# A two-layer decoder trunk: low parts of the weights on VectorE, a third buffer pair, and the keys' factors in the decay tables

## Chip, cores and metric

The kernel runs on one core of a Trainium2 chip. The metric is the device time of one execution in microseconds, the median of three runs.

## The reference

The input x has 512 rows of 1024 float32 numbers. Layer 0 is a gated DeltaNet, layer 1 a gated short convolution, each between two RMS norms and with a residual.

```python
def reference(x, ...):                       # two layers
    for i in range(2):
        h = rms_norm(x, pre_norm_w[i])
        y = gated_deltanet_mixer(h, ...) if i == 0 else short_conv_mixer(h, ...)
        x = x + rms_norm(y, post_norm_w[i])

def gated_deltanet_mixer(h, ...):
    q, k, v, z, b, a = split(h @ w_in)       # 1024 -> 6176; q, k, v after conv of width 4 and SiLU
    q, k = l2_normalize(q), l2_normalize(k)  # 8 heads of 128, each used by two of the 16 value heads
    beta, g = sigmoid(b), -exp(A_log) * softplus(a + dt_bias)
    o = chunked_gated_delta_rule(q, k, v, g, beta)
    return (rms_norm(o, norm_w) * silu(z)) @ w_out          # 2048 -> 1024
# per head and chunk: A = strict(beta k k^T * decay); u, w = solve(I + A, ...);
# v_new = u - w S;  o = q_dec S + (q k^T * decay) v_new;  S = S * sd + k_dec^T v_new

def short_conv_mixer(h, w_in, conv_w, w_out):
    u, b, c, z = split(h @ w_in, 4)          # 1024 -> 4 x 2048
    return (b * conv3(c * u) * silu(z)) @ w_out             # 2048 -> 1024
```

## The kernel before

Every large product is made from three float32r products: an operand is split into a high part (a cast, `hi`) and a low part (the rest, `lo`), and `mm3` (L179) multiplies hi by hi, hi by lo and lo by hi into one PSUM bank. `weights` (L170) brings a tile of weights: a load into `wraw` on SP's DMA queue (three buffers), then `split` (L162), which casts and subtracts into `whi` and `wlo` (two buffers each). `unit` (L184) makes one column block of 128 outputs for all 512 rows, 24 matmuls.

Layer 0 runs 48 such units over w_in (`in_unit`, L469), four of them written out in the start. Their order is the string at L853: keys, queries, z and values of four groups of four heads each. TensorE's order is the program's order; the other engines are ordered by a planner from priorities. The class `Pump` (L61) keeps a clock of planned TensorE time, and every smaller step is a generator (`c_est`, `c_solve`, `c_q`, `c_delta`, `c_gate`, ...) that yields the planned time until its next step; the table `ADJ` (L44) adds a correction to single yields. `at(-16)` gives weight work a priority 16 us ahead of its unit.

The steps that the change touches:

- The decay tables (`decay_tables`, L413) hold exp of differences of the cumulated decay, one 128x512 tile per head, 16 heads. Group 0's are made in SBUF (tiles `gb`), the others from rows that are read back from DRAM (`gt_d`); all are stored to `dt_d` and loaded again where they are used.
- The key step `c_est` (L552) transposes a key tile, makes its squared norm `ss` and the product `kk` of keys with keys in PSUM, and builds E, minus A of the reference. In group 0 VectorE multiplies kk by the factor `nbp` (minus beta over the norm) and by the table in one pass for each of 128 columns (L591); in groups 1 to 3 ScalarE scales kk (L594) and VectorE multiplies by the loaded table `dt` (L596). E has three buffers, tag "E".
- `c_solve` (L609) inverts the triangular blocks: 31 dependent pairs of small VectorE products (L643, L645), then four TensorE steps (L666, L669, L689, L691).
- `c_q` (L702) makes query times key and multiplies it by the table (L719), and makes `qg` on GpSimd (L724). `c_delta` (L730) is the recurrence over four chunks of 128 rows; it makes u from E (L751), scales it into `Vk` and `Vr` on ScalarE (L757, L760) and adds up the output po (L785, L786). `c_gate` (L796) norms and gates the output; its inverse root is `rsqrt` (L196), a start value on VectorE and three Newton rounds of four GpSimd instructions (L204 to L207) on 128x4 numbers.
- The output projection (`out_products`, L929) runs in 16 tiles per half of the heads, with a third pair of weight buffers `wx` in an E buffer for every third tile. The low parts are GpSimd's in the first half and VectorE's in the second.
- `c_norms` (L966) norms two blocks of 128 rows between the layers: two inverse roots on GpSimd, the residual added on GpSimd (L998), transposes, and a split into `hh` and `hl`.

In the split, GpSimd or VectorE takes the low part:

```python
        eng = nc.gpsimd if pool_lo else nc.vector
        eng.tensor_tensor(out=dst_lo, in0=src, in1=dst_hi.bitcast(F32), op=ALU.subtract)
```

Layer 1 (`short_conv`, L1043, then the products of L1099) takes the high parts on ScalarE and the low parts on VectorE throughout.

## Time and profile before

| what | value |
|---|---|
| median of three runs | 1063.34 us (1060.27 to 1063.79) |
| profiled execution | 1058.4 us, span 1056.7 us |
| mean granted TensorE clock | 0.972 of full |
| busy share of the span | TensorE 93%, VectorE 54%, ScalarE 47%, GpSimd 30% |

Times below come from that one execution. A line number names the line of the kernel that issued an instruction; `split` issues all casts and subtractions from L164, L166 and L168, so there the tile's name tells which work it is. Busy time of an instruction that is held up by another engine's use of the memory counts as busy.

### The profile page before, as it was taken

How to read it: one execution, taken by the hardware profiler on the slowest of the kernel's cores; microseconds unless marked ns; L12 is line 12 of the kernel's file. 1: busy time of each engine (PE TensorE's matmuls, PEld its weight loads, DVE VectorE, ACT ScalarE, POOL GpSimd, SP SyncE). 2: the span in 40 equal slices, each digit the busy share in tenths (PEclk: the TensorE clock that was granted, in tenths of full speed). 3: DMA queues.
4: the chain of work that ended last, by engine and by line, in shares of the span. 5: the costliest groups of instructions: out<-in, count | busy, mean ns of one | idle time of the engine just before them, and what ended most of it. 6: DMA issues, size and time to landing. Idle time of an engine off the chain costs nothing.

```text
span 1056.7 us, 14796 instructions
## 1 busy us (share of the span) xinstructions
PE 979.3 (93%) x5430; PEld 807.9 (76%) x5430; DVE 572.7 (54%) x994; ACT 492.5 (47%) x1106; POOL 318.8 (30%) x518
## 2 busy tenths in 40 slices
PE   7984879996999999999998899999999999999997
PEld 5863657884787778777876799888888888888885
DVE  7599979468625882332156776543334434333233
ACT  4473685683646755465654454323223223332123
POOL 6367643455337543546714520000000000000001
PEclk9887889998999999999999999999999999999999
DMA  6243461245225521586555356533333332333222
GB/s 198 83 140 97 144 217 44 60 123 157 61 60 158 162 75 47 161 274 233 178 183 184 95 158 182 152 87 99 100 90 91 100 100 87 93 99 119 85 96 80
DMA packets 170665, 130.78 MB, mean 124 GB/s; under 512 B 6080, under 2 KB 145984, under 8 KB 170208
## 3 DMA queue, kind: packets, MB, share of 16 engines
q1 hardware_dynamic: 170448, 129.73, 40.5%
q8 instruction: 43, 0.70, 0.3%
q14 instruction: 30, 0.25, 0.1%
q10 hardware_dynamic: 144, 0.09, 0.0%
HBM read 117.16 MB, written 12.65 MB: 123 GB/s over the span
## 4 chain that ended last, share of the span: by engine, by line
PE 61%; DVE 17%; DMA 5%; ACT 4%; POOL 4%; issue 3%; POOLq 0%; SPq 0%; DVEq 0%; ACTq 0%
PE pp L180 14%; PE pp L182 13%; PE pp L181 13%; DVE acc L461 4%; DVE tm L643 3%; DVE Na L645 3%; PE pf L181 2%; PE pf L180 2%; PE pf L182 2%; PE pa L180 2%; PE pa L182 2%; PE pa L181 2%; DMA og_d<-ohs 1%; PE u L751 1%; PE po L786 1%
## 5 line engine op out<-in xcount | busy, mean ns | idle before, releaser
L180 PE MATMUL pp<-hh,whi 128*128 128x512 f32 (+1 forms) x928 | 356.7, 384 | 15.9 <-DVE acc L461 6.3
L182 PE MATMUL pp<-hh,wlo 128*128 128x512 f32 (+1 forms) x928 | 347.3, 374 | 3.0 <-POOL wlo L168 1.6
L181 PE MATMUL pp<-hl,whi 128*128 128x512 f32 (+1 forms) x928 | 346.8, 374 | 1.2 <-DVE r L986 1.2
L166 ACT CAST whi<-wraw 128x1024 fp32r<-128x1024 f32 x151 | 158.6, 1050 | 304.6 <-PE pp L181 169.2
L168 DVE TENSOR_TENSOR wlo<-wraw,whi 128x1024 fp32r<-128x1024 f32 x100 | 125.2, 1253 | 175.0 <-ACT whi L166 173.3
L180 PEld LDWEIGHTS pp<-hh,whi 128*128 128x128 f32 x928 | 177.1, 191 | 50.8 <-issue 10.3
L182 PEld LDWEIGHTS pp<-hh,wlo 128*128 128x128 f32 x928 | 176.8, 191 | 37.4 <-POOL wlo L168 3.2
L181 PEld LDWEIGHTS pp<-hl,whi 128*128 128x128 f32 x928 | 177.3, 191 | 30.4 <-DVE r L986 1.4
L168 POOL TENSOR_TENSOR wlo<-wraw,whi 128x1024 fp32r<-128x1024 f32 x55 | 132.3, 2406 | 113.9 <-ACT whi L166 103.0
L1141 POOL TENSOR_TENSOR ob<-ob,ytNa 128x384 f32<-128x384 f32 x2 | 2.1, 1064 | 421.6 <-ACT ob L1140 421.6
L461 DVE SCALAR_TENSOR_TENSOR acc<-pp,col,acc 128x511 f32<-128x511 f32 (+2 forms) x72 | 53.6, 744 | 16.4 <-ACT acc L458 15.5
L645 DVE TENSOR_TENSOR Na<-Na,tm 128x126 f32<-128x126 f32 (+22 forms) x124 | 52.8, 426 | 3.0
L643 DVE TENSOR_TENSOR tm<-Na 128x126 f32<-128x126 f32 (+22 forms) x124 | 47.2, 381 | 3.0
L181 PE MATMUL pf<-wlo,yh 128*128 128x512 f32 x104 | 41.5, 399 | 0.0
L180 PE MATMUL pf<-whi,yh 128*128 128x512 f32 x104 | 41.0, 394 | 0.0
L182 PE MATMUL pf<-whi,yl 128*128 128x512 f32 x104 | 40.8, 392 | 0.0
L1056 DVE TENSOR_TENSOR cu<-pp,us 128x512 f32<-128x512 f32 (+1 forms) x19 | 11.5, 606 | 47.2 <-PE pp L182 47.2
L180 PE MATMUL pp<-xh,whi 128*128 128x512 f32 x64 | 28.6, 447 | 4.3 <-DVE pn L354 3.7
L461 DVE SCALAR_TENSOR_TENSOR acc<-pn,col,acc 128x511 f32<-128x511 f32 (+2 forms) x24 | 26.2, 1100 | 5.7 <-ACT acc L458 5.5
L724 POOL TENSOR_TENSOR qg<-kq,eg 128x512 f32<-128x512 f32 x16 | 22.3, 1392 | 22.6 <-DMA eg<-gt_d 15.4
L182 PE MATMUL pp<-xh,wlo 128*128 128x512 f32 x64 | 27.1, 424 | 0.0
L181 PE MATMUL pp<-xl,whi 128*128 128x512 f32 x64 | 27.0, 421 | 0.0
(297 smaller groups left out, 1540.4 us busy)
## 6 DMA issues: line engine op xcount, KB each, us to landing
wraw<-in_sw_in_dram SPq DMA_DIRECT2D x76, 512.0 KB, 3.9
wraw<-in_w_in_dram SPq DMA_DIRECT2D x47, 512.0 KB, 3.8
wraw<-in_w_out_dram SPq DMA_DIRECT2D x32, 512.0 KB, 3.4
wraw<-in_sw_out_dram SPq DMA_DIRECT2D x16, 512.0 KB, 3.5
eg<-gt_d SPq DMA_DIRECT2D x16, 256.0 KB, 3.6
dtq<-dt_d SPq DMA_DIRECT2D x16, 256.0 KB, 3.5
gb<-gt_d SPq DMA_DIRECT2D x3, 1024.0 KB, 6.1
dt_d<-gb SPq DMA_DIRECT2D x3, 1024.0 KB, 4.3
```

Of the source, the lines that this page charges most:

```text
L166: nc.scalar.copy(dst_hi, src)
L168: eng.tensor_tensor(out=dst_lo, in0=src, in1=dst_hi.bitcast(F32), op=ALU.subtract)
L180: nc.tensor.matmul(ps, lhsT=lh, rhs=rh, start=start, stop=False)
L181: nc.tensor.matmul(ps, lhsT=lh, rhs=rl, start=False, stop=False)
L182: nc.tensor.matmul(ps, lhsT=ll, rhs=rh, start=False, stop=stop)
L461: nc.vector.scalar_tensor_tensor(out=acc[:, s:], in0=ps[:, :T - s], scalar=w(j), in1=acc[:, s:], op0=ALU.mult, op1=ALU.add)
L643: nc.vector.tensor_tensor(out=tv, in0=N[:, i:i + 1, 0:i].to_broadcast([P, w, i]), in1=X[:, m0:, i:i + 1].to_broadcast([P, w, i]), op=ALU.mult)
L645: nc.vector.tensor_tensor(out=X[:, m0:, 0:i], in0=X[:, m0:, 0:i], in1=tv, op=ALU.add)
L724: nc.gpsimd.tensor_tensor(out=qg, in0=qT, in1=eg, op=ALU.mult)
L751: nc.tensor.matmul(u[:, a], lhsT=gs.E[:, 4 * a + c], rhs=X[:, a] if c else gs.nv[a][:, c], start=True, stop=True)
L786: nc.tensor.matmul(po[:, a], lhsT=gs.qkd[a][:, c], rhs=Vr[:, a], start=c == 0, stop=True)
L1056: nc.vector.tensor_tensor(out=cu[:, h:], in0=pc, in1=us, op=ALU.mult)
```

## The change

- `split` takes the low part on VectorE always. The high part is ScalarE's by default; for the units of the input projection and for all of the output projection it is GpSimd's (`hi_eng=nc.gpsimd`).
- Every third call of `weights` uses a third pair of buffers, `third`: in layer 0 from the time that the table of group 1 is stored (it has the same memory, tag "E3"), in layer 1's input projection from a tile of its own. `unit` asks for its weights at priority -20 instead of -16.
- E has two buffers instead of three; the key step of groups 2 and 3 waits until the recurrence of the group two before is done. The table of group 1 waits for the key steps of group 0.
- In the key step ScalarE multiplies the table in place by beta over the norm (`bp`), VectorE multiplies it by kk, 128x512 at a time, and the scaled table is stored to `dt_d`; so the later loads for the queries bring the factor along, and `Vr` is one plain copy of u. E has the other sign, which the solver takes into account (`subtract`, `minus`).
- Between the layers the inverse roots run on VectorE, with three instructions a round instead of four, and the residual is added on VectorE.
- Some 80 entries of ADJ are set anew; of these a few lines are shown.

```diff
@@ -42 +42 @@
 ADJ = {
...
-    "c_solve0:1": -2.5, "c_solve0:2": 1.5, "c_solve1:1": 15.2, "c_solve2:1": 1.5, "c_solve2:2": -6,
...
+    "c_est00:1": -0.2, "c_est01:1": 9.5, "c_est10:1": 2.5, "c_est21:1": -0.5, "c_est30:1": -1, "c_est31:1": 2.6,
+    "c_norms1:1": 10.1, "c_norms1:2": 3.8, "c_q0:0": 42.6, "c_q0:1": -9.5, "c_q1:0": -0.5, "c_q2:0": 9.6,
+    "c_qnorm30:1": -4, "c_solve0:1": 7.5, "c_solve0:2": 0.8, "c_solve1:1": 42.5, "c_solve1:4": 2.5,
+    "c_solve2:1": 7.9, "c_solve2:2": -6, "c_solve3:1": 5.1, "c_solve3:2": -1.5, "c_v00:1": 4.8, "c_v01:1": 5.1,
...
@@ -159 +162 @@
-    def split(dst_hi, dst_lo, src, pool_lo=False, dve_hi=False):
-        if dve_hi:
-            nc.vector.tensor_copy(dst_hi, src)
-        else:
-            nc.scalar.copy(dst_hi, src)
-        eng = nc.gpsimd if pool_lo else nc.vector
-        eng.tensor_tensor(out=dst_lo, in0=src, in1=dst_hi.bitcast(F32), op=ALU.subtract)
-    def weights(src, pool_lo=False, dve_hi=False, store=None):
+    def split(dst_hi, dst_lo, src, hi_eng=None):
+        (nc.scalar.copy if hi_eng is None else hi_eng.tensor_copy)(dst_hi, src)
+        nc.vector.tensor_tensor(out=dst_lo, in0=src, in1=dst_hi.bitcast(F32), op=ALU.subtract)
+    third, n_w = [], [0]
+    def weights(src, hi_eng=None, store=None):
...
         nc.sync.dma_start(out=raw, in_=src)
+        n_w[0] += 1
+        if store is None and third and n_w[0] % 3 == 0:
+            store = [third[0][:, a].rearrange("p (k n) -> p k n", n=n) for a in range(2)]
         hi, lo = store or (wp.tile([P, kk, n], F32R, tag="w" + t, name="w" + t) for t in ("hi", "lo"))
-        split(hi, lo, raw, pool_lo=pool_lo, dve_hi=dve_hi)
+        split(hi, lo, raw, hi_eng)
@@ -181 +185 @@
-    def unit(src, rhs, t=slice(0, T), pool_lo=False, dve_hi=False):
+    def unit(src, rhs, t=slice(0, T), hi_eng=None):
...
         K, m, n = len(rhs), src.shape[2], t.stop - t.start
-        with at(-16):
-            hi, lo = weights(src, pool_lo, dve_hi)
+        with at(-20):
+            hi, lo = weights(src, hi_eng)
...
-    def rsqrt(pool, y, shape, tag, eng=None):
+    def rsqrt(pool, y, shape, tag, vector=False):
...
                                 op0=ALU.mult, op1=ALU.add)
-        eng = eng or nc.gpsimd
         for _ in range(3):
-            eng.tensor_tensor(out=t, in0=r, in1=r, op=ALU.mult)
-            eng.tensor_tensor(out=t, in0=t, in1=y, op=ALU.mult)
-            eng.tensor_scalar(out=t, in0=t, scalar1=-0.5, scalar2=1.5, op0=ALU.mult, op1=ALU.add)
-            eng.tensor_tensor(out=r, in0=r, in1=t, op=ALU.mult)
+            if vector:
+                nc.vector.tensor_tensor(out=t, in0=r, in1=r, op=ALU.mult)
+                nc.vector.scalar_tensor_tensor(out=t, in0=t, scalar=-0.5, in1=y, op0=ALU.mult, op1=ALU.mult)
+                nc.vector.scalar_tensor_tensor(out=r, in0=t, scalar=1.5, in1=r, op0=ALU.add, op1=ALU.mult)
+            else:
+                nc.gpsimd.tensor_tensor(out=t, in0=r, in1=r, op=ALU.mult)
+                nc.gpsimd.tensor_tensor(out=t, in0=t, in1=y, op=ALU.mult)
+                nc.gpsimd.tensor_scalar(out=t, in0=t, scalar1=-0.5, scalar2=1.5, op0=ALU.mult, op1=ALU.add)
+                nc.gpsimd.tensor_tensor(out=r, in0=r, in1=t, op=ALU.mult)
@@ -248 +256 @@
         xt += [dl.tile([P, T], F32, tag="ktok", name="xtk", bufs=4) for _ in range(2)]
-        sq = [dl.tile([P, 4, T], F32, tag="E", name="sqx", bufs=3) for _ in range(2)]
+        sq = [dl.tile([P, 4, T], F32, tag=t, name="sqx", bufs=n) for t, n in (("E", 2), ("E3", 1))]
@@ -345 +353 @@
         g = sm.tile([P, NH, NC], F32, tag="gg", name="gg", bufs=1)
-        gr = dl.tile([NH, 2, T], F32, tag="E", name="gr", bufs=3)
+        gr = dl.tile([NH, 2, T], F32, tag="E", name="gr", bufs=2)
@@ -426 +434 @@
                     nc.scalar.activation(gb, gb, AF.Exp)
-                    nc.sync.dma_start(out=dt_d[h], in_=gb)
...
             hs = slice(4 * g, 4 * g + 4)
-            tag, nb = ("E", 3) if g == 1 else ("zT", 2)
+            tag, nb = ("E3", 1) if g == 1 else ("zT", 2)
@@ -447 +454 @@
         def c_tables(g):
-            while nunit[0] < 10 + 4 * (g - 2):
+            while groups[0].est < 2 or nunit[0] < 10 + 4 * (g - 2):
...
             decay_tables(g)
+            if g == 1:
+                third.append(dl.tile([P, 2, D], F32R, tag="E3", name="w3", bufs=1))
@@ -469 +478 @@
             first = nunit[0] <= 8
-            ps = unit(w_in_v[:, :, ct * P:(ct + 1) * P], xop if first else hT, pool_lo=True,
-                      dve_hi=nunit[0] < 9)
+            ps = unit(w_in_v[:, :, ct * P:(ct + 1) * P], xop if first else hT, hi_eng=nc.gpsimd)
@@ -551 +559 @@
             g = gs.g
-            while not gates_done or (g > 2 and not groups[g - 3].done):
+            while not gates_done or (g > 1 and not groups[g - 2].done):
...
                 gs.epsa = dl.tile([P, 2, NC], F32, tag="epsa", name="epsa")
-                gs.bp, gs.nbp, gs.bpe = (dl.tile([P, 4, NC], F32, tag=n, name=n) for n in ("bp", "nbp", "bpe"))
-                gs.E = dl.tile([P, 16, P], F32, tag="E", name="E", bufs=3)
+                gs.bp, gs.bpe = (dl.tile([P, 4, NC], F32, tag=n, name=n) for n in ("bp", "bpe"))
+                gs.E = dl.tile([P, 16, P], F32, tag="E", name="E", bufs=2)
@@ -576 +584 @@
             h2, g2 = slice(2 * kh, 2 * kh + 2), slice(4 * g + 2 * kh, 4 * g + 2 * kh + 2)
-            nc.vector.scalar_tensor_tensor(out=gs.nbp[:, h2], in0=beta[:, g2], scalar=-1.0,
-                                           in1=rk2.to_broadcast([P, 2, NC]), op0=ALU.mult, op1=ALU.mult)
+            nc.vector.tensor_tensor(out=gs.bp[:, h2], in0=beta[:, g2], in1=rk2.to_broadcast([P, 2, NC]), op=ALU.mult)
@@ -585 +592 @@
                     nc.sync.dma_start(out=dt, in_=dt_d[h])
-                Eh = gs.E[:, 4 * hl_:4 * hl_ + 4]
                 for c in range(NC):
-                    if g < 1:
-                        last_e = nc.vector.scalar_tensor_tensor(out=Eh[:, c], in0=kk[:, c], scalar=gs.nbp[:, hl_, c:c + 1],
-                                                                in1=dt[:, c], op0=ALU.mult, op1=ALU.mult)
-                    else:
-                        nc.scalar.activation(Eh[:, c], kk[:, c], AF.Copy, scale=gs.nbp[:, hl_, c:c + 1])
-                if g >= 1:
-                    nc.vector.tensor_tensor(out=Eh, in0=Eh, in1=dt, op=ALU.mult)
+                    nc.scalar.activation(dt[:, c], dt[:, c], AF.Copy, scale=gs.bp[:, hl_, c:c + 1])
+                last_e = nc.vector.tensor_tensor(out=gs.E[:, 4 * hl_:4 * hl_ + 4], in0=kk, in1=dt, op=ALU.mult)
+                nc.sync.dma_start(out=dt_d[h], in_=dt)
...
                 fence[:] = last_e, last_sq
-            nc.vector.tensor_scalar_mul(gs.bp[:, h2], gs.nbp[:, h2], -1.0)
@@ -642 +643 @@
                                         in1=X[:, m0:, i:i + 1].to_broadcast([P, w, i]), op=ALU.mult)
-                nc.vector.tensor_tensor(out=X[:, m0:, 0:i], in0=X[:, m0:, 0:i], in1=tv, op=ALU.add)
+                nc.vector.tensor_tensor(out=X[:, m0:, 0:i], in0=X[:, m0:, 0:i], in1=tv, op=ALU.subtract)
@@ -656 +657 @@
             yield ((48, 42, 42, 42)[gs.g],)
+            def minus(act, dst, src):
+                if act:
+                    nc.scalar.activation(dst, src, AF.Copy, scale=-1.0)
+                else:
+                    nc.vector.tensor_scalar_mul(dst, src, -1.0)
@@ -671 +678 @@
                     if stage == 0:
-                        copy(Z[b1], ps[h][b1])
+                        minus(h, Z[b1], ps[h][b1])
@@ -692 +699 @@
                     if stage == 0:
-                        copy(V[up, hs], ps[up])
+                        minus(hf, V[up, hs], ps[up])
@@ -756 +763 @@
                 Vr = dl.tile([P, 4, P], F32, tag="Vr", name="Vr", bufs=1)
-                for a in range(4):
-                    nc.scalar.activation(Vr[:, a], u[:, a], AF.Copy, scale=gs.bp[:, a, c:c + 1])
+                nc.scalar.copy(Vr, u)
@@ -828 +834 @@
                 if c == 0:
-                    gs.oh = dl.tile([P, 4, T], F32R, tag="E", name="oh3", bufs=3)
+                    gs.oh = dl.tile([P, 4, T], F32R, tag="E", name="oh3", bufs=2)
@@ -872 +878 @@
                 after(ins, fence[0])
-                split(hh[:, k], hl[:, k], hf, pool_lo=True)
+                split(hh[:, k], hl[:, k], hf)
@@ -884 +890 @@
             start_h(range(8))
-        with at(10):
-            decay_tables(1)
+        pump.add(c_tables(1))
@@ -923 +928 @@
-        wx = dl.tile([P, 2, 2, 512], F32R, tag="E", name="wx", bufs=3)
-        n_w = [0]
-        def out_products(h0, cs, n, pool_lo):
+        def out_products(h0, cs, n, hi_eng):
...
                 with at(-16):
-                    hi, lo = weights(w_out_v[:, h0 + 2 * kk:h0 + 2 * kk + 2, wide[n]], pool_lo=pool_lo,
-                                     store=(wx[:, 0], wx[:, 1]) if n_w[0] % 3 == 2 else None)
-                n_w[0] += 1
+                    hi, lo = weights(w_out_v[:, h0 + 2 * kk:h0 + 2 * kk + 2, wide[n]], hi_eng)
@@ -943 +944 @@
             for n in range(2):
-                banks = out_products(0, cs, n, True)
+                banks = out_products(0, cs, n, nc.gpsimd)
@@ -985 +986 @@
                 nc.vector.tensor_scalar(out=ms, in0=ms, scalar1=1.0 / D, scalar2=EPS, op0=ALU.mult, op1=ALU.add)
-                return rsqrt(sm, ms, [P, n], "rk")
+                return rsqrt(sm, ms, [P, n], "rk", vector=True)
@@ -995 +996 @@
                                                    op0=ALU.mult, op1=ALU.mult)
-                    nc.gpsimd.tensor_tensor(out=y, in0=y, in1=xr[c, n], op=ALU.add)
+                    nc.vector.tensor_tensor(out=y, in0=y, in1=xr[c, n], op=ALU.add)
@@ -1021 +1022 @@
                 cs = (2 * hf, 2 * hf + 1)
-                banks = out_products(8, cs, n, False)
+                banks = out_products(8, cs, n, nc.gpsimd)
@@ -1039 +1040 @@
             tails = {}
+            third[:] = [sp.tile([P, 2, D], F32R, tag="w3", name="w3", bufs=1)]
@@ -1084 +1086 @@
         pump.prio(0)
+        third.clear()
```

## Rows read from the trace of the kernel before

**Rows 1.** Busy time of each engine by stretch, with granted clock and DMA.

```profile
core 0: us, PE busy (x) PEld busy (x) DVE busy (x) ACT busy (x) POOL busy (x), PEclk, DMA share, GB/s
...
60.00:125.00 65.00, 43.00 (x184) 34.22 (x183) 63.06 (x128) 36.29 (x103) 48.24 (x76) 0.82 0.40 119
125.00:180.00 55.00, 45.13 (x354) 35.16 (x354) 46.35 (x96) 40.02 (x83) 22.13 (x21) 0.94 0.44 138
...
240.00:280.00 40.00, 27.80 (x181) 21.47 (x180) 37.58 (x81) 18.34 (x47) 19.45 (x24) 0.91 0.39 114
280.00:340.00 60.00, 60.00 (x433) 51.96 (x432) 22.22 (x54) 34.91 (x112) 27.65 (x66) 1.00 0.32 93
...
560.00:622.00 62.00, 52.98 (x303) 45.98 (x301) 45.10 (x66) 29.95 (x57) 33.56 (x80) 0.92 0.47 143
622.00:1057.00 435.00, 427.72 (x2033) 354.63 (x2033) 178.72 (x215) 133.84 (x184) 4.12 (x4) 1.00 0.35 105
```

**Rows 2.** TensorE's waits over the span: total us, times, longest us.

```profile
PE kq L712 <- ACT ktok L568: 9.1, 1, 9.1
PE pot L819 <- ACT of L814: 8.8, 1, 8.8
...
PE pp L180 <- ACT zT L528: 5.4, 2, 5.0
...
PE pp L182 <- POOL wlo L168: 1.6, 2, 1.0
```

**Rows 3.** Groups of instructions over the span: busy us, mean ns.

```profile
L166 ACT CAST whi<-wraw 128x1024 fp32r<-128x1024 f32 x151 | 158.6, 1050 | 304.6 <-PE pp L181 169.2 <-issue 64.4 <-PE pf L182 38.6
L168 POOL TENSOR_TENSOR wlo<-wraw,whi 128x1024 fp32r<-128x1024 f32 x55 | 132.3, 2406 | 113.9 <-ACT whi L166 103.0 <-PE tok L536 5.1 <-DVE whi L164 3.3
L168 DVE TENSOR_TENSOR wlo<-wraw,whi 128x1024 fp32r<-128x1024 f32 x100 | 125.2, 1253 | 175.0 <-ACT whi L166 173.3
L461 DVE SCALAR_TENSOR_TENSOR acc<-pp,col,acc 128x511 f32<-128x511 f32 (+2 forms) x72 | 53.6, 744 | 16.4 <-ACT acc L458 15.5
...
L656 POOL COPY E<-Nb 32x512 f32<-32x512 f32 x8 | 4.9, 608 | 12.8 <-DVE Nb L650 12.6
```

**Rows 4.** Groups of VectorE and GpSimd from 60 to 125 us.

```profile
L461 DVE SCALAR_TENSOR_TENSOR acc<-pn,col,acc 128x511 f32<-128x511 f32 (+2 forms) x15 | 17.5, 1176 | 0.0
L645 DVE TENSOR_TENSOR Na<-Na,tm 128x126 f32<-128x126 f32 (+20 forms) x27 | 15.1, 560 | 0.4
...
L168 POOL TENSOR_TENSOR wlo<-wraw,whi 128x1024 fp32r<-128x1024 f32 x5 | 12.4, 2475 | 1.1 <-ACT whi L166 1.1
L168 POOL TENSOR_TENSOR hl<-hf,hh 128x512 fp32r<-128x512 f32 x8 | 11.2, 1410 | 3.5 <-ACT hh L166 3.5
```

**Rows 5.** Timeline of GpSimd, then of VectorE: start us, us, instruction.

```profile
240.41 0.20 POOL L204 TENSOR_TENSOR ft<-fr 128x4 f32<-128x4 f32 x1
...
247.56 2.34 POOL L168 TENSOR_TENSOR wlo<-wraw,whi 128x1024 fp32r<-128x1024 f32 x1
...
253.22 0.20 POOL L207 TENSOR_TENSOR fr<-fr,ft 128x4 f32<-128x4 f32 x1
...
247.29 0.26 DVE L645 TENSOR_TENSOR Na<-Na,tm 128x96 f32<-128x96 f32 x1
247.58 2.45 DVE L643 TENSOR_TENSOR tm<-Na 128x115 f32<-128x115 f32 x1
```

**Rows 6.** Timeline of GpSimd in the norms between the layers.

```profile
562.52 0.19 POOL L204 TENSOR_TENSOR rkt<-rkr 128x2 f32<-128x2 f32 x1 [31.41 <-DVE rkr L200]
...
566.63 0.20 POOL L207 TENSOR_TENSOR rkr<-rkr,rkt 128x2 f32<-128x2 f32 x1
567.69 7.32 POOL L998 TENSOR_TENSOR ytNa<-ytNa,xr 128x512 f32<-128x512 f32 x4 [0.87 <-DVE ytNa L996]
```

**Rows 7.** Group 2's key step, group 0's end, group 2's first use, a table load.

```profile
L594 ACT ACTIVATE E<-kk,nbp x16: 346/379/409, 209.7 to 227.1; 128x128 f32<-128x128 f32 x16
...
230.56 0.39 PE L786 MATMUL po<-Vr,qkd 128*128 128x128 f32 x2
...
L751 PE MATMUL u<-nv,E x8: 275/275/377, 379.6 to 380.9; 128*128 128x128 f32 x8
...
dt<-dt_d SPq DMA_DIRECT2D x12, 256.0 KB, 2.9
```

24 rows, old and new, of the table ADJ are left out of this document.

## The prediction

> **What bounds the kernel now.** I read the stages first: the table of busy time by stretch [rows 1]. From 622 us to the end TensorE is busy for 427.72 of 435 us at full clock, and the missing 7.3 us are the drain behind its last product. Nothing in the change can shorten that part, so the whole question lies in the first 622 us, the DeltaNet layer and its output projection. There the idle time of TensorE sits in four stretches: 22.0 us in 60 to 125, 9.9 in 125 to 180, 12.2 in 240 to 280 and 9.0 in 560 to 622 (length less busy time). In the same stretches the granted clock falls to 0.82, 0.94, 0.91 and 0.92 of full, so they pay twice. VectorE is busy for 63.06 of 65 us in the first and 37.58 of 40 in the third, but for only 22.22 of 60 in 280 to 340: it limits in patches, not on average.
>
> Second, TensorE's own waits [rows 2]. The long ones end at ScalarE (a key copy that holds a PSUM bank, 9.1 us; the scaled output before the gate's transpose, 8.8; the gate z, 5.4). For a low part of a weight it waits only 1.6 us in all. So the weights are not late as such. What is late are short jobs that stand behind long ones.
>
> Third, why they are late. When GpSimd subtracts a low part, VectorE's small solver product stands still: one that takes 0.26 us takes 2.45 at 247.58, and GpSimd's pass runs from 247.56 for 2.34 us [rows 5]. GpSimd pays as well: its chain of small Newton steps for the output norm starts at 240.41 and ends at 253.42, with two of these long passes between its links; TensorE's 8.8 us wait ends right behind it. In 60 to 125 this is summed up in [rows 4]: 15 convolution passes from SBUF take 17.5 us where those from PSUM take 0.744 each [rows 3], so 6.3 us too much; 27 solver updates take 15.1 us where 0.27 each would be 7.3, so 7.8 too much. That is 14.1 us of stretching beside 23.6 us of GpSimd passes (wlo and hl), or 0.6 us for each us.
>
> **The change part by part.**
>
> *The weights' split.* By the code 44 units of the input projection and 16 tiles of the output projection move their low part from GpSimd (2.406 us each) to VectorE (1.253), and these 60 and 16 more move their high part from ScalarE (1.050; four from VectorE) to GpSimd [rows 3]. No row shows that cast on GpSimd. From below, its copy of 512 elements takes 0.608, and an equal time for 1024 is the least; from above stands its own subtraction, 2.406. I take twice the copy, 1.2 us, because the cast too reads one operand. Per unit the chain cast, subtract becomes 1.2 + 1.25 = 2.45 us instead of 1.05 + 2.41 = 3.46, and ScalarE loses 1.05 us per unit.
>
> For VectorE in 60 to 125: five low parts (6.3 us) and eight of the normalised input come to it, each of these half as long, 0.63 (5.0), in sum 11.3 us. GpSimd's passes fall from 23.6 to 6.0 us (five casts), so 0.6 x 17.6 = 10.6 us of stretching go: +0.7 for VectorE.
>
> *Keys' factors in the decay tables.* In the first group 16 small VectorE passes, 0.27 us each if they are like the solver's, become four products of 512 elements (0.63): 4.3 become 2.5 us, and half of the 1.8 saved lies in 60 to 125. In the others ScalarE scales the table instead of the PSUM product, as many passes as before; only it can now start before the product is there. The recurrence's four scaled copies become one, on ScalarE, off the state's own path. So VectorE's account of 60 to 125 closes at -0.2; with the five casts gone from ScalarE's queue, where the key copy stands, I take -2. Bounds: +10 (no stretching goes) and -10 (all 14.1 us of it go, so -3.7 on VectorE, and half of the 11.7 us by which the clock of 0.82 shortens these 65). Twelve more 256 KB stores go through the in-order SP queue, behind which the next table and weight loads stand; and as two table buffers serve four heads, the third load of a group waits until the first store has landed. A load of that size takes 2.9 us [rows 7]; three groups that pay it in full are 8.7. I put +1 on it, since the recurrence that needs the tables starts much later (next but one), bounds 0 and +9.
>
> *125 to 180.* The 5.4 us for z ends at ScalarE; a cast less on its queue gives 1 us. The solver's TensorE steps, which wait in the rest of the stretch, are placed later for groups 0 and 1, with weight products before them. I take -4 of 9.9, bounds 0 and -8; VectorE's added passes, six or seven low parts, fit into its 8.7 us of idle time here.
>
> *240 to 280.* The Newton chain loses 2 x (2.34 - 1.2) = 2.3 us directly. More matters that the key buffer E goes from three to two: the key step of group 2 now waits for the end of group 0's recurrence. It ran from 209.7 to 227.1; that recurrence ends at 230.6 [rows 7]. So the solver's 62 dependent steps behind it move by some 21 us, into the stretch where VectorE is busy a third of the time. It costs nothing, as group 2's recurrence first reads E at 379.6. I take -7 of 12.2 and the clock's 3.6 (0.09 of 40), bounds 0 and -13.
>
> *Third buffer pair.* It gives a unit's time of reserve. Directly it can save the 1.6 us of [rows 2]; I take -2 with the shorter chain, bounds 0 and -6 (with what is late in stretches not named here). In the second layer nothing waits.
>
> *Norms between the layers.* Twelve GpSimd steps from 562.52 to 566.83 become nine on VectorE; at the same 0.28 us a step that is 2.5 instead of 4.3. Four residual adds of 7.32 us [rows 6] become four VectorE passes of 0.63, 2.5 us. Twice, once per half of the rows, that is some 13 us of chain; the stage has only 9.0 us idle and 5 us of lost clock (0.08 of 62). The second half's casts go to GpSimd, which is otherwise free there. I take -6, bounds 0 and -12.
>
> *Sum:* -2 - 4 - 7 - 2 - 6 + 1 = -20. The profiled execution took 1058.4 us (span 1056.7 and 1.7 around it), so 1038.4; the median of the runs lies 4.9 above that execution, which gives **1043 us**.
>
> **The rivals.**
>
> *The exchange is empty.* If a GpSimd cast blocks VectorE as the subtraction did, a unit takes 1.2 + 1.25 = 2.45 us of the two engines' common time instead of 2.41, and ScalarE's cast, which stopped nobody, is wasted. Then only norms and placement remain, half as strong: 1054 to 1066, say 1060. For it speaks the stretched row of [rows 5]; against it, that VectorE then waits 1.2 us at a time and not 2.4, and that the small chains pass sooner. The Trainium skill states this rule on the page "SBUF — State Buffer", section "SBUF: two separate sides": GpSimd and a VectorE instruction with two SBUF inputs take a shared port pair exclusively for a whole instruction, and ScalarE never waits on anyone. The trace agrees in its first half (0.26 us became 2.45). By "GPSIMD Engine Reference", section "Engine selection", one-input work runs near line rate; at that page's 1.2 GHz 1024 elements are an estimated 0.85 us, by which the stretching in 60 to 125 would fall by 1 us more.
>
> *VectorE becomes the bound (slower).* Place: the stretches where it has no idle time, above all 60 to 125. It decides if the cast takes long: the first stage breaks even where 0.6 x (23.6 - 5c) = 11.3 - 0.9, at c = 1.25 us, barely over my 1.2. In 60 to 125, 125 to 180 and 240 to 280 some 15 low parts and 8 of the input bring 24 us; if half of it delays TensorE, the time is 1075, if all, 1087.
>
> *The placement does more.* If the steps placed later take away nearly all 53 us of idle time in the four stretches, beyond the waits for VectorE, 1005 to 1022, say 1015. Against it: 60 to 125 has no VectorE time to spare.
>
> **How the numbers follow.** Forecast (1022 to 1054) 0.55; more gain 0.13; empty exchange 0.14; slower 0.18. A change under 0.3% (3.2 us) can't be told from none, so the same is 1060.1 to 1066.5. Faster: 0.55 + 0.13 and 0.05 of the empty exchange, 0.73; same 0.09; slower 0.18. The range 1018 to 1070 leaves out about half of the biggest gain and some two thirds of the slower case, 0.2 together.
>
> **What would show it.** Right: low parts on VectorE near 1.25 us and casts on GpSimd near 1.2; solver steps no longer stretched to 2.4; the wait of 8.8 us gone; group 2's key step behind 231 us; the stretch of the norms without GpSimd; the second layer at the same 435 us. Wrong: casts over 1.25 us, VectorE full to 180 us with more TensorE idle time than 22.0 and 9.9, a key or query step that waits for a table load, or new waits of TensorE at the moved steps.

## The result, and the profile after

The changed kernel takes **1029.99 us** (median; 1027.09 to 1035.51), the kernel before on the same chip 1063.36; the ratio is 0.9698 with an interval of 0.9652 to 0.9744, so some 33 us faster. The forecast was 1043 in a range of 1018 to 1070. The profiled execution took 1028.76 us, 9.6 less than the 1038.4 of the sum. Its busy time by stretch, with the columns of [rows 1]:

```profile
60.00:125.00 65.00, 47.17 (x217) 38.30 (x218) 60.01 (x127) 42.27 (x126) 38.13 (x69) 0.84 0.53 162
125.00:180.00 55.00, 52.66 (x403) 42.34 (x403) 49.37 (x110) 32.21 (x82) 13.62 (x20) 1.00 0.51 154
240.00:280.00 40.00, 37.34 (x180) 30.82 (x179) 31.32 (x78) 24.09 (x83) 13.40 (x41) 0.96 0.41 119
...
560.00:592.00 32.00, 29.14 (x211) 27.14 (x210) 30.81 (x74) 16.33 (x31) 0.00 (x0) 0.95 0.61 169
592.00:1027.00 435.00, 428.07 (x2040) 354.72 (x2038) 178.07 (x217) 133.69 (x185) 4.08 (x4) 0.99 0.36 104
```

The last 435 us are as before, so all of the gain lies ahead of them. TensorE's idle time (length less the first column) is 17.8, 2.3, 2.7 and 2.9 us in the four stretches that had 22.0, 9.9, 12.2 and 9.0. The first hardly looks better, but stretches of equal clock time no longer hold equal work. So I laid both traces' matmuls out in order, gave each the usual interval of its line in the trace of before, and read when each kernel reached the same sum (worked out, no view of the profile):

```
time in before, us       125   180   240   300   560   622
time after, same work  119.3 164.8 224.2 277.1 534.0 592.0
gain so far              5.7  15.2  15.8  22.9  26.0  30.0
```

Half of the gain is made by 180 us. How far one execution can be trusted is shown by e10 below, in which every engine has the same order. The same sums from its trace, of an execution of 1033.82 us, give gains of 3.2, 12.3, 13.1, 19.4, 22.7 and 24.4 at these six points; so a single stretch is known to some 3 us. TensorE's remaining waits in 60 to 125 (what waited, for what; us in all, times, longest):

```profile
PE pp L184 <- POOL w L166: 8.4, 1, 8.4
PE pp L184 <- DVE pn L362: 5.8, 1, 5.8
PE pp L186 <- DVE w L167: 3.9, 1, 3.9
```

The costs that the forecast had to estimate, in groups by line (count | busy us, mean ns), from the lists of VectorE and GpSimd:

```profile
L166 POOL CAST whi<-wraw 128x1024 fp32r<-128x1024 f32 x51 | 62.1, 1219 | 94.0 <-PE pp L185 60.8 <-PE pa L186 16.2 <-DMA wraw<-in_w_out_dram 6.5
L166 POOL CAST w<-wraw 128x1024 fp32r<-128x1024 f32 x25 | 28.6, 1142 | 43.9 <-PE pp L185 25.0 <-PE pa L186 8.0 <-DVE rkr L210 5.9
...
L646 DVE TENSOR_TENSOR Na<-Na,tm 128x126 f32<-128x126 f32 (+22 forms) x124 | 39.4, 317 | 2.7
L644 DVE TENSOR_TENSOR tm<-Na 128x126 f32<-128x126 f32 (+22 forms) x124 | 37.5, 302 | 2.9
L470 DVE SCALAR_TENSOR_TENSOR acc<-pn,col,acc 128x511 f32<-128x511 f32 (+2 forms) x24 | 17.6, 745 | 5.5 <-ACT acc L467 5.3
```

The cast takes 1.14 to 1.22 us in the mean, as taken (1.2); its median is 1.045, and a few that VectorE holds up are longer. The solver's pairs took 426 + 381 ns in the kernel before and take 317 + 302: 124 pairs, 23 us of VectorE's time.

```profile
L645 DVE TENSOR_TENSOR Na<-Na,tm 128x126 f32<-128x126 f32 (+22 forms) x124 | 52.8, 426 | 3.0
L643 DVE TENSOR_TENSOR tm<-Na 128x126 f32<-128x126 f32 (+22 forms) x124 | 47.2, 381 | 3.0
```

The convolution passes that took 1.1 us in the kernel before are back at 745 ns. A cast does hold VectorE up, but shortly. In the changed kernel's timeline a product that is free at 0.28 takes 1.01 us beside a cast of 1.14, where one beside a subtraction took 2.45 [rows 5]:

```profile
113.39 1.14 POOL L166 CAST whi<-wraw 128x1024 fp32r<-128x1024 f32 x1
...
113.35 0.28 DVE L644 TENSOR_TENSOR tm<-Na 128x126 f32<-128x126 f32 x1
113.67 1.01 DVE L646 TENSOR_TENSOR Na<-Na,tm 128x126 f32<-128x126 f32 x1
```

### The profile page after: what moved, and what is told of

Same layout as the page of the kernel before. It is cut to its first block, busy times and chain, and to the rows that moved or that the text cites. A ratio compares the mean times of both kernels' runs of the same rounds, so it can differ in the third digit from the quotient of the medians.

```text
span 1026.6 us, 14732 instructions
## 1 busy us (share of the span) xinstructions
PE 974.4 (95%) x5430; PEld 805.7 (78%) x5430; DVE 612.3 (60%) x1100; ACT 420.6 (41%) x1002; POOL 235.4 (23%) x446
## 4 chain that ended last, share of the span: by engine, by line
PE 75%; DVE 9%; DMA 6%; ACT 4%; issue 3%; POOL 2%; SPq 0%; POOLq 0%; DVEq 0%; ACTq 0%
PE pp L184 17%; PE pp L186 17%; PE pp L185 17%; PE pf L185 3%; PE pf L184 2%; PE pf L186 2%; PE pa L186 2%; PE pa L185 2%; PE pa L184 2%; PE u L758 2%; DVE wlo L167 1%; DMA gb<-gt_d 1%; PE po L792 1%; PE psn L772 1%; PE p L748 1%
## 5 line engine op out<-in xcount | busy, mean ns | idle before, releaser
L184 PE MATMUL pp<-hh,whi 128*128 128x512 f32 (+1 forms) x624 | 239.2, 383 | 5.1 <-DVE acc L470 2.1
L185 PE MATMUL pp<-hl,whi 128*128 128x512 f32 (+1 forms) x624 | 233.3, 374 | 1.0 <-DVE r L987 1.0
L186 PE MATMUL pp<-hh,wlo 128*128 128x512 f32 (+1 forms) x624 | 233.3, 374 | 0.0
L167 DVE TENSOR_TENSOR wlo<-wraw,whi 128x1024 fp32r<-128x1024 f32 x115 | 141.4, 1229 | 135.5 <-ACT whi L166 110.1
L166 ACT CAST whi<-wraw 128x1024 fp32r<-128x1024 f32 x64 | 67.2, 1050 | 189.8 <-PE pp L185 112.2
L186 PEld LDWEIGHTS pp<-hh,wlo 128*128 128x128 f32 x624 | 118.8, 190 | 22.2
L185 PEld LDWEIGHTS pp<-hl,whi 128*128 128x128 f32 x624 | 119.1, 191 | 21.1 <-DVE hl L167 1.2
L184 PE MATMUL pp<-hh,w 128*128 128x512 f32 (+1 forms) x304 | 116.1, 382 | 0.0
L186 PE MATMUL pp<-hh,w 128*128 128x512 f32 (+1 forms) x304 | 113.2, 373 | 1.1 <-DVE w L167 1.1
L185 PE MATMUL pp<-hl,w 128*128 128x512 f32 (+1 forms) x304 | 113.2, 372 | 0.0
L166 POOL CAST whi<-wraw 128x1024 fp32r<-128x1024 f32 x51 | 62.1, 1219 | 94.0 <-PE pp L185 60.8
L167 DVE TENSOR_TENSOR w<-wraw,w 128x1024 fp32r<-128x1024 f32 x50 | 62.6, 1252 | 33.8 <-ACT w L166 31.7
L186 PEld LDWEIGHTS pp<-hh,w 128*128 128x128 f32 x304 | 57.3, 189 | 12.4 <-DVE w L167 1.5
L184 PEld LDWEIGHTS pp<-hh,w 128*128 128x128 f32 x304 | 57.5, 189 | 10.3 <-issue 0.4
```

Of the source, the lines that this page charges most:

```text
L166: (nc.scalar.copy if hi_eng is None else hi_eng.tensor_copy)(dst_hi, src)
L167: nc.vector.tensor_tensor(out=dst_lo, in0=src, in1=dst_hi.bitcast(F32), op=ALU.subtract)
L184: nc.tensor.matmul(ps, lhsT=lh, rhs=rh, start=start, stop=False)
L185: nc.tensor.matmul(ps, lhsT=lh, rhs=rl, start=False, stop=False)
L186: nc.tensor.matmul(ps, lhsT=ll, rhs=rh, start=False, stop=stop)
```

## The experiments

Each starts from the changed kernel unless it says otherwise; a loss in us is the difference of its ratio to 0.9698, times the 1062 us of before. Lines of "..." in a diff stand for edited lines that are not shown.

**The split's engines put back, and the high parts on ScalarE.**

In e1 the low parts are GpSimd's and the high parts ScalarE's (the first four VectorE's) where the kernel before has them so; in e2 only the high parts move, to ScalarE:

```diff
e1
-        nc.vector.tensor_tensor(out=dst_lo, in0=src, in1=dst_hi.bitcast(F32), op=ALU.subtract)
+        (lo_eng or nc.vector).tensor_tensor(out=dst_lo, in0=src, in1=dst_hi.bitcast(F32), op=ALU.subtract)
-            ps = unit(..., xop if first else hT, hi_eng=nc.gpsimd)
+            ps = unit(..., xop if first else hT, hi_eng=nc.vector if first else None, lo_eng=nc.gpsimd)
-                split(hh[:, k], hl[:, k], hf)
+                split(hh[:, k], hl[:, k], hf, lo_eng=nc.gpsimd)
...
e2
-            ps = unit(..., xop if first else hT, hi_eng=nc.gpsimd)
+            ps = unit(..., xop if first else hT)
-                banks = out_products(8, cs, n, nc.gpsimd)
+                banks = out_products(8, cs, n, None)
...
```

> The changed kernel with the split's engines put back: low parts of the input projection, of the normalised input and of the first half of the output projection on GpSimd, high parts on ScalarE (the first four units' on VectorE). All else stays as changed: steps placed anew, third pair, factors in the tables, norms. If the exchange of engines is the main source of the 33 us (theory 'exchange'): 1045 to 1055 us, solver products of VectorE stretched to over 2 us again, mean of the solver's two products back above 0.37 us. If the new placement is the main source (theory 'placement'): 1025 to 1036 us. If it is the third pair: also 1025 to 1036 us.

> The changed kernel with all high parts on ScalarE and all low parts on VectorE, so GpSimd casts nothing. If a GpSimd cast stops VectorE as its subtraction did (the rival 'empty exchange' in its weaker form): 5 to 10 us faster, 1020 to 1025 us, since some 76 casts of 1.2 us no longer meet VectorE. If ScalarE's queue is the dearer place, because 76 casts of 1.05 us stand there behind table passes and gate work: 1032 to 1040 us.

Measured: e1 1057.18 us, ratio 0.9952 (0.9938 to 0.9965), a loss of 27 us. e2 1056.86, 0.9947 (0.9924 to 0.9970), 26 us. Both lie above every value expected. In e1 the first stage is far worse (same columns as above), with a wait of TensorE of 14.8 us for the first tile of the third pair:

```profile
60.00:125.00 65.00, 40.70 (x178) 32.46 (x179) 57.08 (x113) 44.21 (x120) 43.95 (x72) 0.76 0.40 121
125.00:180.00 55.00, 46.29 (x307) 36.23 (x307) 42.28 (x100) 38.22 (x80) 25.00 (x21) 0.88 0.58 183
```

```profile
PE pp L184 <- DVE w L166: 14.8, 1, 14.8
```

VectorE is busy for less than in the changed kernel (57.08 of 65, then 42.28 of 55), and TensorE idles 24.3 and 8.7 us. But these 65 us hold less work. For the TensorE work that the changed kernel does from 60 to 125, e1 takes from 59 to 140, and there VectorE is busy for 68.8 us against 60.0, with 13 more of the solver's products done:

```profile
59.00:140.00 81.00, 50.57 (x218) 40.15 (x218) 68.78 (x135) 53.15 (x138) 55.33 (x82) 0.79 0.45 137
```

So the sum of VectorE's busy time doesn't tell the two kernels apart. By equal work e1 has lost 20 of its 27 us by 161 us. In e2 GpSimd casts nothing, and the solver runs almost free (groups by line):

```profile
L644 DVE TENSOR_TENSOR tm<-Na 128x126 f32<-128x126 f32 (+22 forms) x124 | 34.2, 276 | 2.8
L646 DVE TENSOR_TENSOR Na<-Na,tm 128x126 f32<-128x126 f32 (+22 forms) x124 | 33.3, 269 | 2.9
```

A ScalarE cast holds VectorE up by nothing that shows: 19 products that run beside one, and beside no GpSimd instruction, take 259 ns in the mean, and 176 beside neither take 252 (worked out from e2's trace, no view). GpSimd's casts cost these products 9 us in all ((302 + 317 - 276 - 269) x 124). Still e2 loses 26 us; in its trace 8 by 161 us and 33 by 424. TensorE's waits from 55 us on that end at ScalarE come to 28 us against 9 in the changed kernel (those at GpSimd to 0 against 8, at VectorE to 30 against 20), so a good part of it is lost in ScalarE's queue; what the displaced order adds is not separated. The empty exchange falls, and so does the idea that the cast would be as well on ScalarE.

**Old places, and the new split alone in the kernel before.**

e3 has the table ADJ of the kernel before and nothing else put back. Of the 83 entries in the changed table, 24 have another value than before and 17 are new, and three are gone; the other 42 stayed, so fewer were set anew than the "some 80" above. e7 is the kernel before with the new split alone (and `pool_lo` on in the second half of the output projection):

```diff
e7, against the kernel before
...
-        eng = nc.gpsimd if pool_lo else nc.vector
-        eng.tensor_tensor(out=dst_lo, in0=src, in1=dst_hi.bitcast(F32), op=ALU.subtract)
+        (nc.gpsimd.tensor_copy if pool_lo else nc.scalar.copy)(dst_hi, src)
+        nc.vector.tensor_tensor(out=dst_lo, in0=src, in1=dst_hi.bitcast(F32), op=ALU.subtract)
...
```

> The changed kernel with the table of corrections of the kernel before, so only the placement of the steps goes back. Theory 'placement': 1045 to 1060 us, with the waits of TensorE at the solver's and the gate's steps back. Theory 'exchange': 1030 to 1040 us.

> The kernel before with the new split alone: casts on GpSimd, low parts on VectorE in the units of the first layer and in the output projection, and the low parts of the normalised input on VectorE; places, two buffer pairs, tables and norms as before. Theory: split and places are worth something only together. The solver's TensorE steps stand where the solver's products on VectorE were just done with the old split, and VectorE has now more work ahead of them, so TensorE waits for them as in the changed kernel with the old places: 1070 to 1090. Rival, the forecast's addition: the split alone takes 10 to 15 us away by less stretching of VectorE, 1047 to 1055.

Measured: e3 1083.25 us, 1.0200 (1.0179 to 1.0220); e7 1083.68, 1.0202 (1.0178 to 1.0226). Both are 21 us slower than before, and e3 is slower than either theory had it. TensorE's longest waits, of e3 and then of e7:

```profile
PE pz L670 <- DVE X L651: 29.7, 4, 10.9
PE pot L822 <- ACT of L817: 11.3, 3, 5.8
```

```profile
PE pz L661 <- DVE X L648: 19.7, 3, 10.4
PE pot L814 <- ACT of L809: 16.1, 5, 6.1
```

The solver's first TensorE step (pz) now comes before VectorE has finished X. By equal work e7, in which only the split is new, is 16.4 us *ahead* of the kernel before at its 173 us; at 316 us 1.5 are left, at 627 it is 21.4 behind. So the split by itself lets TensorE run ahead. But the solver is not ahead as far: its products for group 1 end at 170.7 us in e7, at 177.9 in the kernel before, so 7 us sooner, and at the old place TensorE stands for them:

```profile
172.64 1.92 PE L661 MATMUL pz<-X,E 32*32 32x32 f32 x64 [10.44 <-DVE X L648]
```

In the changed kernel these products end later still, at 185.5; there the step stands at 194, behind more weight products (the entry `c_solve1:1` goes from 15.2 to 42.5), and doesn't wait. That is what the new places do for the split at this step. Long waits of e7 stand also at the gate (pot) and at the norms between the layers, 10.8 us in one. The old split at the new places (e1) is 27 us slower than the changed kernel and 5 faster than the one before, and the norms alone give 4.6 (e11, below). So split and places give little or a loss alone.

**The third pair: used late, only in the output projection, or its table freed early.**

```diff
-        if store is None and third and n_w[0] % 3 == 0:
+        if store is None and third and n_w[0] % 3 == 0 and n_w[0] > 3:
e5
+        if store is None and third and n_w[0] % 3 == 0 and kk == 2:
e9, in decay_tables
-                        if g == 1:
+                        if g == 0:
                             after(e, fence[1])
```

The first is e4. In e9 the fence falls away: with g == 0 the function has returned before this line. In e5 `kk == 2` holds for the output projection's tiles alone.

> The changed kernel, but the third buffer pair is first used at the sixth weight tile instead of the third, so that no unit waits for the store of group 1's table, which has the same memory. In the changed kernel TensorE waits 8.4 us for the cast into that pair and 3.9 us for its low part, at 72 to 86 us. If this wait is a loss of its own: 1017 to 1024 us and no wait of over 3 us there. If VectorE, busy for 60 of the 65 us from 60 to 125, is the bound there and the wait is only where its lateness shows: 1027 to 1032 us, with the idle time moved behind 90 us.

> The changed kernel, but the third pair of weight buffers serves the output projection alone, as before; the units of both layers' input projections take the two pairs. If the third pair is the small reserve of the forecast (2 us), the median is 1030 to 1034 us, and the waits of TensorE for a low or high part grow by a few us in all. Rival: with a chain of GpSimd cast and VectorE subtraction that stands behind other VectorE work, the third pair is what lets the units run ahead; then waits for weights appear in many stretches of the first 500 us and the median is 1040 or more. In the second layer both expect no difference in the 435 us.

> The changed kernel without the fence that holds one of the sixteen exponentials of group 1's table until the second key step's squares are made. In the changed kernel that one runs at 74.38, alone, between two table loads of 1.28 us; the store of the table and with it the third weight pair's first use stand behind it, and TensorE waits 8.8 and 4.5 us at that tile. The planner then also pulls group 1's key products on VectorE ahead of the solver's. If that wait is a loss of its own, the median falls by 4 to 10 us, to 1020 to 1026. Rival, after the run that used the pair later: VectorE and the order of its work set the end of the first 180 us, and what is gained before 90 us is given back behind it: 1028 to 1045.

These go back to the largest wait left, 8.4 us (and 3.9 behind it). One exponential of group 1's table is held by a fence and runs alone at 74.38 (ScalarE's timeline of the changed kernel); the store behind it delays the cast into the third pair, which has the same memory (GpSimd's timeline):

```profile
54.63 4.50 ACT L448 ACTIVATE gb<-gb,nG 128x128 f32<-128x128 f32 x15
61.48 1.28 ACT L472 ACT_TABLE_LOAD   x1
73.08 1.28 ACT L448 ACT_TABLE_LOAD   x1
74.38 0.40 ACT L448 ACTIVATE gb<-gb,nG 128x128 f32<-128x128 f32 x1
74.80 1.28 ACT L472 ACT_TABLE_LOAD   x1
```

```profile
79.19 1.48 POOL L166 CAST w<-wraw 128x1024 fp32r<-128x1024 f32 x1 [1.63 <-DMA dt_d<-gb]
```

Measured: e4 1037.27 us, 0.9761 (0.9730 to 0.9792), 7 us lost; e9 1037.18, 0.9759 (0.9734 to 0.9785), 6 lost; e5 1039.83, 0.9798 (0.9772 to 0.9824), 11 lost. The intervals of e4 and e9 touch that of the changed kernel, which ends at 0.9744, but not that of its repetition e10, which ends at 0.9722. e4 lies above both of its expected ranges. In e4 and e9 the wait is gone, and by equal work they are 13 and 15 us ahead where the changed kernel is at 93 us. At its 161 us they are 6.4 and 0.7 behind, at 204 us 13.2 and 6.1. In their place stand other waits for VectorE; in e9:

```profile
PE pp L184 <- DVE acc L470: 8.5, 3, 4.5
PE pp L184 <- DVE pn L362: 6.3, 1, 6.3
```

That wait was therefore no loss that its removal gives back: my theory of 1017 to 1026 fell twice. In e5 low parts are late in many places (`PE pp L186 <- DVE wlo L167: 11.6, 6, 3.5` in its waits).

**The norms and the keys' factors put back, and the norms alone in the kernel before.**

e8 also stores group 0's tables where they are made, as before; e11 is e6 the other way round, in the kernel before.

```diff
e6
-                return rsqrt(sm, ms, [P, n], "rk", vector=True)
+                return rsqrt(sm, ms, [P, n], "rk")
-                    nc.vector.tensor_tensor(out=y, in0=y, in1=xr[c, n], op=ALU.add)
+                    nc.gpsimd.tensor_tensor(out=y, in0=y, in1=xr[c, n], op=ALU.add)
e8
...
-                    nc.scalar.activation(dt[:, c], dt[:, c], AF.Copy, scale=gs.bp[:, hl_, c:c + 1])
-                last_e = nc.vector.tensor_tensor(out=gs.E[:, 4 * hl_:4 * hl_ + 4], in0=kk, in1=dt, op=ALU.mult)
-                nc.sync.dma_start(out=dt_d[h], in_=dt)
+                    if g < 1:
+                        last_e = nc.vector.scalar_tensor_tensor(out=Eh[:, c], in0=kk[:, c], scalar=gs.bp[:, hl_, c:c + 1], in1=dt[:, c], ...)
+                    else:
+                        nc.scalar.activation(Eh[:, c], kk[:, c], AF.Copy, scale=gs.bp[:, hl_, c:c + 1])
+                if g >= 1:
+                    nc.vector.tensor_tensor(out=Eh, in0=Eh, in1=dt, op=ALU.mult)
...
-                nc.scalar.copy(Vr, u)
+                for a in range(4):
+                    nc.scalar.activation(Vr[:, a], u[:, a], AF.Copy, scale=gs.bp[:, a, c:c + 1])
```

> The changed kernel, but the inverse roots and the residual between the layers are GpSimd's as before. If the term of the forecast (6 us) is right, the median is 1034 to 1038 us and TensorE's busy share from 560 us to the start of the second layer falls by about 5 us of work. Rival: the other work of that stretch hides the longer chain, or GpSimd's casts for the second half hide behind it: 1029 to 1032. Second rival: with these casts on the same engine the residuals of 7 us delay the weights as well, and it costs 8 to 12 us: 1038 to 1042.

> The changed kernel, but with the keys' factors applied as before: in the first group VectorE multiplies by factor and table in 16 small passes, in the others ScalarE scales the product of the keys, the tables are stored without the factor, and the recurrence scales four copies. If this part is worth what the forecast put on it (about nothing, one us of it on VectorE in 60 to 125), the median is 1029 to 1034. Rival: the first group's key step sets the end of 60 to 125, and its 16 small passes and the four scaled copies per chunk are a good part of what the change gave: 1038 to 1045, with the loss before 150 us and in the recurrences.

> The kernel before with the norms between the layers on VectorE alone, nothing else. Put back in the changed kernel they cost 12 us, all of it at one wait for the second block's transposes. If they are worth that by themselves, the median is 8 to 12 us under before, 1050 to 1055; if the forecast's term holds, 6 us, 1055 to 1058; rival: in the kernel before the work of the second half of the output projection hides most of the chain, and it gives 0 to 3 us.

Measured: e6 1042.18 us, 0.9812 (0.9787 to 0.9837), 12 lost, by equal work all of it behind 529 us, where one wait stands out: TensorE stands 13.6 us before the transposes of the norms, behind four residual adds on GpSimd of 6.27 us together and two chains of 12 steps:

```profile
PE pxr L1011 <- DVE hs L1005: 13.6, 1, 13.6
```

```profile
552.23 6.27 POOL L999 TENSOR_TENSOR ytNa<-ytNa,xr 128x512 f32<-128x512 f32 x4 [0.87 <-DVE ytNa L997]
558.46 0.20 POOL L212 TENSOR_TENSOR rkt<-rkr 128x1 f32<-128x1 f32 x1
```

e11 1058.06, 0.9957 (0.9941 to 0.9973): in the kernel before the same edit gives 4.6 us. On VectorE a step takes 0.16 us, not the 0.28 of the forecast. e8 1043.62, 0.9832 (0.9809 to 0.9855), 14 lost, but not where I had put it: until 295 us it is up to 3 us ahead, and 8 us of the loss appear at one step of group 2's solver, for which VectorE is 5.7 us late (the granted clock is 0.76 from 295 to 316 us there):

```profile
306.35 3.67 PE L702 MATMUL pdw<-X,E 64*64 64x64 f32 x32 [5.68 <-DVE X L690]
```

**The scale: the same program again, and places off by 1 us.**

```diff
e10, in unit
-        with at(-20):
+        with at(-16):
e12
-    "c_delta0:0": -2.5, "c_delta0:10": 2.1, "c_delta0:14": 4, "c_delta0:3": -1, "c_delta0:9": 1.3,
+    "c_delta0:0": -1.5, "c_delta0:10": 1.1, "c_delta0:14": 5, "c_delta0:3": -2, "c_delta0:9": 2.3,
...
```

> The changed kernel with the units' weights asked for 16 us ahead instead of 20, as before. The forecast put nothing on this edit. If each order of the steps is about as good as another, the median stays at 1028 to 1034. Rival: the table of corrections is set for one order of the engines' queues, and any edit that shifts the order costs about what the third pair, the keys' factors and the norms cost when they were put back one at a time: 1036 to 1044.

> The changed kernel with nothing but its table of places disturbed: each of the 83 corrections is moved by 1 us, in turn up and down. It is the scale for the runs that put one part back: each of these also moves the steps around it. If the order need not be exact to 1 us, the median stays within 3 us of the changed kernel (1027 to 1033), and the 10, 12 and 14 us that the third pair, the norms and the keys' factors cost when put back are the parts' own. If the order is set to within 1 us, it costs 6 to 15 us (1036 to 1045), spread over many short waits, and a part's price read by putting it back alone is an upper bound that holds such displacement.

Measured: e10 1029.32 us, 0.9696 (0.9670 to 0.9722). The edit leaves the order on every engine as it was, so this is a repetition, and agrees to 0.0002. e12 1053.88, 0.9919 (0.9887 to 0.9951): 23 us lost by moving 83 corrections by 1 us each, more than the 15 that were the most expected. Waits of TensorE in e12, and GpSimd's timeline at the longest wait for the gate's transpose (pot):

```profile
PE pot L825 <- ACT of L820: 16.9, 5, 6.5
PE pp L184 <- POOL w L166: 10.4, 1, 10.4
```

```profile
434.26 0.20 POOL L213 TENSOR_TENSOR ft<-ft,fy 128x4 f32<-128x4 f32 x1
437.77 1.26 POOL L731 TENSOR_TENSOR qg<-kq,eg 128x512 f32<-128x512 f32 x1 [3.32 <-DMA eg<-gt_d]
439.00 0.19 POOL L214 TENSOR_SCALAR ft<-ft 128x4 f32<-128x4 f32 x1
439.13 1.04 POOL L166 CAST whi<-wraw 128x1024 fp32r<-128x1024 f32 x1
440.13 0.20 POOL L215 TENSOR_TENSOR fr<-fr,ft 128x4 f32<-128x4 f32 x1
```

Between two 0.2 us steps of the output norm's root stands a pass that waits 3.3 us for a table load. Nothing of the work has changed; only what stands behind what in a queue. By equal work e12 has lost 4 us at 161 us, 12 at 295 and 25 at 529. The waits for pot come to 4.0 us in the changed kernel and 16.9 here, so short waits there are one thing that the places buy.

So e1 reads in two parts, for its 27 us in all are hardly more than the 23 of e12. By 161 us e1 has lost 20. A displacement of the order has cost 4 by then in e12, and between 1 and 9 in the others that keep the new split on its engines (e3, e4, e5, e8, e9). So at least some 11 of the 20 are the split's, and e7 shows 16 in the same stretch from the other side. Its later loss, some 9 us, is no more than a displacement costs. The 11 and 14 us of e5 and e8 lie within that too and can't be read as these parts' own prices.

## Why the prediction was right, and what was mis-sized

- **The bound.** Right: the second layer stayed at 435 us, all gain lies in the first layer and its projection, and VectorE's stretched short jobs are short again.
- **The split, 60 to 180 us.** The terms were -2 and -4; by equal work the gain is 5.7 by 125 us and 9.5 in 125 to 180 (3.2 and 9.1 in e10's trace). The second is outside its own bound of -8, which left out the 3.3 us that the granted clock of 0.94 cost there (it is 1.00 after). These two terms are 9.2 of the 9.6 us between sum and trace; they are what was mis-sized. The prices in them held (cast, low part; the low parts of the input take 0.82, not 0.63). What was wrong is the place of the longest wait. The forecast put the 9.1 us for the key copy down to ScalarE's queue, from which five casts go. But ScalarE itself had just stood 5.7 us for a convolution pass of VectorE (ScalarE's timeline of the kernel before):

```profile
105.43 0.63 ACT L463 ACTIVATE kq<-acc 128x512 f32<-128x512 f32 x1 [5.66 <-DVE acc L461]
107.42 0.58 ACT L568 COPY ktok<-tok 128x512 f32<-128x512 f32 x1
```

  So most of this wait was VectorE's. TensorE's waits in 60 to 180 for the key copy, for the convolved keys (tok on kq, 8.1 us, which the forecast doesn't name) and for z come to 22.6 us before; with the split alone (e7, 58 to 163 us, the same work) 3.6 are left, in the changed kernel 0.8. They are not the split's alone to remove: in e1, with the old split, new places and the other parts leave 5.9. The balance of VectorE's busy time, with break-even at a cast of 1.25 us, was close by its own numbers (the casts in 60 to 125 took 1.19 to 1.24). It left out the short steps of the norms and the keys' factors, which were stretched too (0.88 and 0.80 us before, 0.17 and 0.16 in e7, some 4 us in all), and it doesn't say what TensorE waits for. How long single short steps are held up differs clearly between the two splits (2.45 us beside a subtraction, 1.01 beside a cast).
- **240 to 280 us.** -7 forecast, 7.1 by equal work from 240 to 300. Group 2's key step runs at 238 us, behind the end of group 0's recurrence, and TensorE doesn't wait for its solver; "at no cost" is right, though without much reserve: in e8 the same solver is 5.7 us late. The forecast named only the two low parts between the links of the Newton chain. Two `qg` passes stood there as well, each behind a wait for its table (kernel before):

```profile
244.27 1.38 POOL L724 TENSOR_TENSOR qg<-kq,eg 128x512 f32<-128x512 f32 x1 [1.16 <-DMA eg<-gt_d]
251.52 1.42 POOL L724 TENSOR_TENSOR qg<-kq,eg 128x512 f32<-128x512 f32 x1 [1.44 <-DMA eg<-gt_d]
```

  With the waits they are 5.4 us of the chain's 13, more than the low parts' 4.7, and the change leaves such passes between the links.
- **Third pair and the rest to 560.** -2 forecast, 3.1 by equal work. Right in size; new is the 8.4 us wait for its memory, which the list of what would show it wrong named as a new wait, and whose removal in e4 and e9 gains nothing.
- **Norms.** -6 forecast; 4.0 by equal work, 4.6 in e11. The forecast's sum of 13 us counts one inverse root for each half of the rows where there are two. That e6 loses 12 I put down to the work placed ahead of it, which no run separates.
- **Table stores.** +1 forecast. None of TensorE's waits of 1.5 us or more ends at a table load itself, but the longest one left for the gate stands behind two. It ends behind a Newton chain from 219.66 to 230.66 us, in which two `qg` passes wait 3.38 and 1.15 us for their tables (changed kernel; the first of them, then TensorE):

```profile
223.52 1.29 POOL L731 TENSOR_TENSOR qg<-kq,eg 128x512 f32<-128x512 f32 x1 [3.38 <-DMA eg<-gt_d]
231.11 1.26 PE L825 MATMUL pot<-ident,of 128*128 128x128 f32 x4 [3.62 <-ACT of L820]
```

  The sign named as wrong shows on the other engines too. ScalarE's scaling in the key step waits 7.1 us for its tables (nothing before), VectorE's query products 8.9 (2.4), `qg` 20.6 in all (15.4). So the term is not nothing; how much of these waits the added stores cause stays open.
- **Rivals.** The empty exchange had the mechanism right: a cast also holds VectorE up. The Trainium skill, "SBUF — State Buffer", section "SBUF: two separate sides", says so for a GpSimd instruction that reads there, against a VectorE instruction with two inputs from there, and says that ScalarE never waits on anyone. The trace agrees with the first by the 1.01 us beside a cast, and with the second by the 259 ns beside a ScalarE cast in e2. The rival's price was wrong, since a cast holds for half as long. The slower case did come, in e3 and e7, at 1083 us and by another mechanism than the one I gave: not VectorE full to the end, but TensorE's solver steps placed ahead of VectorE's work. "The placement does more" was half right: I gave the places 0.13 for 1015, and the runs show that without them the rest of the change, and the split alone, are a loss of 21 us. My sum treated split and places as terms that add; they don't. That the total came within 13 us rests on both being in the change.

What stays open: how much of the 33 us another table of places for the old split would have given, since no run tuned one, and whether a cast holds VectorE for less because it is shorter or because it reads one input.

## What to carry to other kernels

Where one engine's small dependent steps are held up by another's long passes, look at the length of the single pass and not only at the sum of busy time. Exchanging a 2.4 us subtraction for a 1.1 us cast cut GpSimd's passes of the split from 155 to 91 us, but what the solver's products lose beside them from 32 to 9 us (against the 276 + 269 ns of e2), and TensorE was 16 us ahead by 173 us (e7). Follow a long wait past the engine at which it ends: that engine may itself have stood for another. Such a move shifts when each engine is done, so the order written for the old timing has to be set anew with it, or the gain turns into a loss (e7, e3). And in a kernel ordered to the microsecond, putting one part back measures the part and the displaced order together: run a control that only shifts the order before reading such a loss as the part's price, and don't expect a visible wait to be worth its length.

## What the runs showed of the hardware that was not expected

- GpSimd's small steps stand still beside VectorE's passes as well as the other way round. In the changed kernel a step on 128x4 numbers that takes 0.20 us alone took 1.79 at 67.39, while VectorE ran passes without a gap. A cast at 542.7 took 5.13 us, while VectorE ran four residual adds and two low parts.
- A GpSimd pass with two operands and 512 columns (`qg`, 1.29 us) held a VectorE product for 1.42 us at 110.75; the three longest of the solver's products left in the changed kernel (1.42, 1.41 and 1.22 us) stand beside it and not beside a cast alone.
- ScalarE's table load took 1.28 us each time; the exponential held by a fence cost two of them.
